# Convolution in-projections of a hybrid decoder trunk by Strassen's algorithm, with mixer outputs kept in DRAM

## Chip, cores and metric

The kernel runs on one core of a Trainium2 chip. The metric is the device time of one execution in microseconds. All inputs and outputs are float32 in DRAM.

## What is computed

A trunk of four layers is applied to one prompt of 1024 rows and to 8 decoding sequences of 4 rows each (model width 1024). Every layer modulates its input by vectors computed from a condition c (`adaln`), runs a mixer and closes with a gate, a residual and a layer norm. Layers 0 and 3 mix by a gated short convolution, layer 1 by an RG-LRU block, layer 2 by differential attention. What the change touches is the first product of the convolution layers, `u @ w_in`.

```python
def adaln(c, w, b):
    m = (jax.nn.silu(c) @ w + b)[:, None, :]
    shift, scale, gate = jnp.split(m, 3, axis=-1)
    return shift, scale, gate

def short_conv_mixer(u, buf, w_in, conv_w, w_out):
    h, bg, cg, z = jnp.split(u @ w_in, 4, axis=-1)
    y, new_buf = causal_dwconv(cg * h, buf, conv_w)
    return (jax.nn.silu(z) * bg * y) @ w_out, new_buf
...
    up = xp * (1.0 + scp) + shp
    us = xs * (1.0 + scs) + shs
...
    xp = layer_norm(DEEPNORM_ALPHA * xp + gtp * op, ln_g[i], ln_b[i])
```

## The kernel before

Activations lie transposed: 8 units (`u[k]`) of 128 features by NT = 1056 columns, 1024 of the prompt and 32 of the sample rows. Each number is held as two float32r parts, hi and lo, side by side in one unit, and every weight likewise. A product of two such numbers is three matmuls (hi·hi, w hi·u lo, w lo·u hi), so one output tile over 8 feature blocks is 24 matmuls (`gemm_chunk`, L123). The columns go in three chunks, `CH` = 384, 384 and 288.

`conv_layer` loops over 8 output blocks i. Each block takes four slices of 128 columns of `w_in`, in the order q = 2, 0, 3, 1 (cg, h, z, bg). `part` runs one chunk of one slice and finishes it: ScalarE copies cg out of PSUM (L397), VectorE multiplies (p, L405), ScalarE and VectorE do the convolution with width 3 (L413, L415), ScalarE applies silu (L429), VectorE forms the two last products (L431, L432), and `split` writes the result as hi and lo into `y[i]` (L92, L93), which the out-projection reads. In layer 0, block 0 goes chunk by chunk over all four slices, because its input columns come chunk by chunk.

Weights come by `load_w` (through `conv_weights`): a DMA of 512 KB on SP's queue into a raw buffer (L106, ring of two), a cast by ScalarE (hi, L107) and a subtraction by VectorE (lo, L108) into a ring of two weight tiles. All DMAs shown here go through SP's queue, in order. After each slice `filler` may put out one `ada_piece`: four DMAs of 512 KB from `w_ada` (L185, in the same raw ring) with 16 matmuls (L191), a copy and four transposes, for the gates of this and the next layer. In layer 0 there are 8 such pieces, in layer 3 none. After the layer, `boundary` runs the out-projection (tile `op`), the residual and the norm.

PSUM has 8 banks in four groups (P 3, Q 1, R 3, U 1), handed out in turn by `deal`. A scheduler sets the order of instructions per engine at build time from the order in the code, the buffers and its own costs; each engine then works its queue in order.

Of the kernel before, what the change touches and what calls it, by code (L numbers as in the profile page):

```python
# [21 lines left out]
T = 1024  # L22
NB = 8
# [9 lines left out]
CH = [(0, 384), (384, 384), (768, 288)]  # L33
TILES = [[(0, 128), (128, 128), (256, 128)], [(0, 128), (128, 128), (256, 128)], [(0, 128), (128, 128), (256, 32)]]
NPG = 16
SAMPLE_COST = NB * (32 * 430 + 8 * 890 + 620 + 4 * 430 + 16 * 400 + 300 + 300.0)
LAM_INIT = 0.8 - 0.6 * math.exp(-0.3 * 2)

# [6 lines left out]
class Trunk:  # L45
# [324 lines left out]
    def conv_weights(self, l, y, s):  # L370
        wv = self.a["a_w_in"][l // 3].rearrange("(k p) f -> p k f", p=128)
        i, q = s // 4, (2, 0, 3, 1)[s % 4]
        dst = None
        if l == 0 and s in (2, 3):
            dst = y[KB - 4 + s]
# [4 lines left out]
    def conv_layer(self, l, u, y, filler, wts=()):  # L380
# [4 lines left out]
        first = len(wts) > 0  # L385

        def ld(s):
            if s < 4 * KB and s not in wts:
                wts[s] = self.conv_weights(l, y, s)

        def part(i, q, c, wt, cg, yc, sz, p, psv):
            c0, n = CH[c]
            npr = min(n, T - c0)
            ps = self.gemm_chunk(wt, u, c, f"in{l}_{i}_{q}_{c}")
            if q == 2:
                cg[c] = cg.get(c) or self.sm(f"cg{l}_{i}_{c}")
                nc.scalar.copy(cg[c][:, :n], ps[:, :n])  # L397
            elif q == 0:
                yc[c] = yc.get(c) or self.sm(f"yc{l}_{i}_{c}")
                t = p[c] = self.sm(f"p{l}_{i}_{c}")  # L400
# [10 lines left out]
                w = [self.pv[:, i, R_CW + 3 * j + k : R_CW + 3 * j + k + 1] for k in range(3)]  # L411
                o = yc[c]
                nc.scalar.mul(o[:, :npr], t[:, 0:npr], w[0])  # L413
                for k in (1, 2):
                    nc.vector.scalar_tensor_tensor(  # L415
                        o[:, :npr], t[:, k : k + npr], w[k], o[:, :npr], ALU.mult, ALU.add
                    )
                if npr < n:
                    ov = o[:, npr:n].rearrange("p (b t) -> p b t", b=NB)
                    nc.vector.tensor_scalar(ov, psv[:, :, 0:4], w[0], None, ALU.mult)  # L420
                    for k in (1, 2):
                        nc.vector.scalar_tensor_tensor(ov, psv[:, :, k : k + 4], w[k], ov, ALU.mult, ALU.add)
                    nc.gpsimd.tensor_copy(stage[:, i, 0:2], t[:, npr : npr + 2])
                    nc.gpsimd.tensor_copy(
                        stage[:, i, 2:18].rearrange("p (b t) -> p b t", b=NB), psv[:, :, 4:6]
                    )
# [8 lines left out]
        ld(0)  # L435
        for i in range(KB):
            cg, yc, sz, p = {}, {}, {}, {}
# [3 lines left out]
            if first and i == 0:  # L441
                for s in range(4):
                    ld(s)
                for c in range(3):
                    for s, q in enumerate((2, 0, 3, 1)):
                        part(i, q, c, wts[s], cg, yc, sz, p, psv)
                ld(4)
                for s in range(4):
                    wts.pop(s)
                    filler(s, 4 * KB)  # L450
                continue
            pair = l == 3 and i == 0
            if pair:
                for s in range(3):
                    ld(s)
                for c in range(3):
                    for s, q in enumerate((2, 0)):
                        part(i, q, c, wts[s], cg, yc, sz, p, psv)
                for s in range(2):
                    wts.pop(s)  # L460
            for k, q in enumerate((2, 0, 3, 1)):
                if pair and k < 2:
                    continue
                s = 4 * i + k
                ld(s + 1)
                wt = wts.pop(s)
                if k < 3:
                    t, d = (("cg", cg), ("yc", yc), ("sz", sz))[k]
                    for c in range(3):
                        d[c] = self.sm(f"{t}{l}_{i}_{c}")  # L470
                for c in range(3):
                    part(i, q, c, wt, cg, yc, sz, p, psv)
                filler(s, 4 * KB)
# [849 lines left out]
    def run(self):  # L1323
# [65 lines left out]
        self.conv_layer(0, A, B, filler_for((0, 4), (0, 5), 1), wts)  # L1389
        boundary(0, a["a_w_out"][0], B, A)  # L1390
        if self.layers > 1:
            ct.__exit__(None, None, None)
# [33 lines left out]
            cms = [ct] + cms  # L1426
            boundary(2, a["d_w_out"][0], A, B)
        if self.layers > 3:
            self.conv_layer(3, A, B, filler_for())
# [84 lines left out]
```

## Time and profile before

| what | us |
|---|---|
| median of 3 runs (lowest to highest) | 2508.14 (2506.17 to 2513.81) |
| the profiled execution's own time | 2500.39 |
| span of its profile | 2498.6 |
| mean granted TensorE clock in it | 0.991 |
| layer 0, in-projections (tile in, first to last start) | 34 to 448, with ada pieces between |
| layer 3, in-projections | 2033 to 2384 |

One execution was profiled; its span runs from the first to the last instruction, and 1.8 us of its time lie outside. PE is TensorE's matmul side, PEld its weight loads, which overlap; DVE is VectorE, ACT ScalarE, POOL GpSimd, SP the engine whose queue issues DMAs. L123 is line 123 of the kernel before. A matmul's own duration overlaps with the next one's, so distances between starts tell what one costs. "Idle before" is the time an engine stood still ahead of an instruction, with what released it.

### The profile page before, as it was taken

What the parts mean: (1) busy time and instruction counts of PE and PEld (TensorE: products, weight loads), DVE (VectorE), ACT (ScalarE), POOL (GpSimd) and SP (SyncE); (2) the same over time, 40 slices, a digit from 0 to 9 for tenths busy, and PEclk for the clock granted to TensorE, in tenths of its full rate; (3) what the DMA queues carried; (4) which work ended last, traced back from release to release, by engine and by line L of the source; (5) the groups of instructions that cost most, each with busy time, mean ns of one, the idle gap of its engine ahead of it and who ended that gap; (6) DMA issues with size and microseconds to landing.
All of it is one profiled execution on the core that took longest, in us unless ns stands there. A gap on an engine that the chain in (4) does not pass through costs nothing.

```text
span 2498.6 us, 41729 instructions
## 1 busy us (share of the span) xinstructions
PE 2419.9 (97%) x16142; PEld 2102.1 (84%) x16142; DVE 1210.6 (48%) x2702; ACT 894.3 (36%) x1837; POOL 195.4 (8%) x330
## 2 busy tenths in 40 slices
PE   8999999999999999999999989988998999999997
PEld 5999999998888897777778966666776999999997
DVE  5323232466466546333333257777874552332355
ACT  4212221246455424112222257677762342222210
POOL 0000000001001000000000023232200000000000
PEclk9999999999999999999999999999999999999999
DMA  9223222433444524344588478899877321111132
GB/s 328 78 85 93 77 78 86 132 100 105 143 133 128 154 70 150 95 153 153 176 276 275 149 216 257 262 267 251 273 253 233 99 68 51 43 44 51 43 118 84
DMA packets 276715, 364.13 MB, mean 146 GB/s; under 512 B 15085, under 2 KB 192622, under 8 KB 276518
## 3 DMA queue, kind: packets, MB, share of 16 engines
q1 hardware_dynamic: 276518, 361.48, 46.3%
q8 instruction: 127, 2.08, 0.4%
q14 instruction: 70, 0.57, 0.1%
HBM read 313.94 MB, written 47.48 MB: 145 GB/s over the span
## 4 chain that ended last, share of the span: by engine, by line
PE 86%; DMA 9%; DVE 2%; ACT 2%; issue 1%; SPq 1%; POOL 0%; DVEq 0%; ACTq 0%; POOLq 0%
PE in L123 30%; PE op L123 15%; PE qk L796 10%; PE xb L123 4%; PE z L123 4%; PE skt L1131 4%; DMA kp<-cache_k 3%; PE ada L191 2%; PE zz L123 2%; PE S L912 2%; PE sps L1112 2%; PE g L628 2%; PE sacc L1171 2%; PE pv L1005 2%; DMA vp<-cache_v 1%; DMA tok<-kd 1%
## 5 line engine op out<-in xcount | busy, mean ns | idle before, releaser
L123 PEld LDWEIGHTS in<-ua,wi 128*128 128x128 f32 x4392 | 707.7, 188 | 22.5 <-issue 14.3
L123 PE MATMUL in<-ua,wi 128*128 128x384 f32 (+1 forms) x4392 | 722.4, 324 | 1.3 <-ACT wi L107 0.7
L796 PE MATMUL qk<-wq,ua 128*128 128x512 f32 x1152 | 289.6, 402 | 0.5 <-ACT qkr L800 0.5
L796 PEld LDWEIGHTS qk<-wq,ua 128*128 128x128 f32 x1152 | 211.4, 189 | 61.4 <-issue 11.4
L1131 PE MATMUL skt<-ident,kp 128*128 128x128 f32 x1024 | 143.8, 276 | 15.3 <-DMA kp<-cache_k 13.9
L1131 PEld LDWEIGHTS skt<-ident,kp 128*128 128x128 f32 x1024 | 116.1, 141 | 41.8 <-issue 11.6
L964 ACT ACTIVATE P<-S,rr 128x512 f32<-128x512 f32 (+2 forms) x192 | 111.1, 586 | 32.7 <-DVE rr L952 22.6
L912 PE MATMUL S<-ks,qhl 128*128 128x512 f32 (+2 forms) x384 | 109.3, 388 | 9.1 <-ACT P L964 8.8
L1135 DVE COPY sk<-skt 128x512 f32<-128x512 f32 x128 | 86.8, 686 | 58.5 <-PE skt L1131 38.0
L283 DVE SCALAR_TENSOR_TENSOR r<-op,gate,xr 128x384 f32<-128x384 f32 (+1 forms) x96 | 54.2, 569 | 121.5 <-PE op L123 85.4
L431 DVE TENSOR_TENSOR sz<-in,sz 128x384 f32<-128x384 f32 (+1 forms) x48 | 25.1, 524 | 176.9 <-PE in L123 176.5
L1135 ACT COPY sk<-skt 128x512 f32<-128x512 f32 x128 | 75.1, 590 | 78.7 <-PE skt L1131 51.9
L123 PEld LDWEIGHTS z<-ub,wrz 128*128 128x128 f32 x576 | 92.5, 188 | 11.7 <-issue 10.1
L123 PE MATMUL zz<-ua,wz 128*128 128x384 f32 (+1 forms) x576 | 102.0, 329 | 0.0
L123 PEld LDWEIGHTS zz<-ua,wz 128*128 128x128 f32 x576 | 92.2, 188 | 7.1 <-issue 7.0
L123 PE MATMUL z<-ub,wrz 128*128 128x384 f32 (+1 forms) x576 | 98.2, 326 | 0.0
L123 PEld LDWEIGHTS xb<-ub,wrx 128*128 128x128 f32 x504 | 81.0, 188 | 12.7 <-issue 9.2
L123 PE MATMUL xb<-ub,wrx 128*128 128x384 f32 (+1 forms) x504 | 87.9, 328 | 0.0
L191 PE MATMUL ada<-wada,ct 128*32 128x512 f32 x384 | 83.0, 624 | 3.6 <-DMA wada<-w_ada 2.4
L1171 PE MATMUL sacc<-vp,pt 128*32 128x256 f32 x1024 | 73.9, 395 | 12.6 <-DMA vp<-cache_v 10.8
L123 PE MATMUL op<-ub,ua 128*128 128x384 f32 (+1 forms) x504 | 85.5, 326 | 0.0
L123 PE MATMUL op<-ua,ub 128*128 128x384 f32 (+1 forms) x504 | 85.3, 325 | 0.0
(415 smaller groups left out, 3733.3 us busy)
## 6 DMA issues: line engine op xcount, KB each, us to landing
kp<-cache_k SPq DMA_DIRECT2D x128, 512.0 KB, 4.7
vp<-cache_v SPq DMA_DIRECT2D x128, 512.0 KB, 4.9
wada<-w_ada SPq DMA_DIRECT2D x96, 512.0 KB, 4.7
xa<-xat SPq DMA_DIRECT2D x64, 192.0 KB, 2.2
xr<-xa SPq DMA_DIRECT2D x64, 192.0 KB, 3.6
wi_2r<-a_w_in SPq DMA_DIRECT2D x16, 512.0 KB, 4.1
wi_0r<-a_w_in SPq DMA_DIRECT2D x16, 512.0 KB, 4.2
wi_3r<-a_w_in SPq DMA_DIRECT2D x16, 512.0 KB, 4.1
```

The lines of the kernel that those rows point to most:

```text
L123: nc.tensor.matmul(ps[:, :n], wt[:, wp, k], self.ucols(units[k], up, c), start=i == 0, stop=i == 3 * KB - 1)
L191: nc.tensor.matmul(ps[c : c + 32, :], self.ct[:, k], wts[k // 2][:, k % 2], start=k < 4, stop=k >= 4, tile_position=(0, c),)
L283: nc.vector.scalar_tensor_tensor(r[:, :npr], ps[:, :npr], gate[:, d, 0:1], xt[:, :npr], ALU.mult, ALU.add)
L628: nc.tensor.matmul(ps[:, :n], wt[:, wp, q, k, m * 128 : (m + 1) * 128], self.ucols(y[2 * i + k], up, c), start=j == 0, stop=j == 5,)
L796: nc.tensor.matmul(ps, u[k][:, c0 : c0 + 128], wq[n, k // 2][:, wp, k % 2], start=i == 0, stop=i == 3 * KB - 1)
L912: nc.tensor.matmul(st[:, o : o + w], qs[h, g][:, part, s, 128 * qj : 128 * qj + 128], ks[h][:, s, l0 : l0 + w], start=part == 0, stop=part ...
L964: nc.scalar.activation(p[:, o : o + w], x["S"][s][i][:, :w], AF.Exp, scale=-1.0, bias=rr[:, 6 + s : 7 + s], accum_out=rr[:, c : c + 1])
L1005: nc.tensor.matmul(x["pv"], x["w"][kb // 4][:, j : j + 128], V[h][:, kb], start=kb == 0, stop=kb == qb)
L1112: nc.tensor.matmul(ps[32 * g : 32 * g + 32, :n], qbs[b % 2][:, 2 * g + hl], kt[hl][:, g], start=hl == 0, stop=hl == 1, tile_position=(0, 3 ...
L1131: nc.tensor.transpose(tp[:, 128 * g : 128 * g + 128], pg[j][:, 128 * h : 128 * h + 128], ident)
L1135: e(kt[:, :, 128 * j : 128 * j + 128], tp.rearrange("p (g t) -> p g t", g=4))
L1171: nc.tensor.matmul(acc[32 * g : 32 * g + 32, :], pts[0][:, 128 * (p % 4) + 32 * g : 128 * (p % 4) + 32 * g + 32], v[:, 256 * g : 256 * g + ...
```

## The change

The in-projections of blocks 1 to 7 are done by Strassen's algorithm (Winograd's form with 7 products). Two slices of one block make a pair: kind 0 is (cg, h), kind 1 is (z, bg). The 2x2 matrices are: the two slices by two halves of the input features (4 blocks each), and the two halves of the features by two halves of the columns (HB = 528). Seven steps take the place of eight; one step is two halves of 12 matmuls with 264 columns, accumulated into PSUM banks X (two), Y (two) and Z (two).

- Block 0 stays direct. It stores its result to DRAM (`yd[0]`, L496). While it runs, `conv_sums` forms the column-side sums of the units (GpSimd adds hi and lo back together, L393; VectorE subtracts, L397 to L400) and splits them into `y`, which is free until the end.
- `conv_pair_weights` loads the two raw slices (L425), casts the first one whole (`direct`, wa), forms four sums on VectorE (L435 to L438) and splits them (`early`, `late`, `last`; casts L413, subtractions L414). These six stages of the next pair are put out after steps 0, 1, 2, 3, 5 and 6 of a pair.
- `pair` runs the seven steps (matmuls L603), copies banks out on ScalarE (p1, u2, p5, u3, L586) and adds on VectorE (L610, L622) and GpSimd (L619).
- There are 13 pairs per layer; (z, bg) of block 7 stays direct, in four chunks of 264. In that last half block `ret` reads the seven stored results back (L677) and splits them into `y`.
- `swap(True)` closes the pool of temporaries and opens one for the pairs; `swap(False)` reverses it.

Block 7's result goes straight into `y[7]`. Lines in the diff and the orders below are those of the changed kernel.

```diff
@@ -372,12 +373,89 @@
+    def conv_sums(self, l, u, e, d):
...
+        for x in (u[d], u[d + 4]):
+            t = self.xct(f"cs{l}_{d}_{len(b)}")
+            xf = x.bitcast(F32)
+            nc.gpsimd.tensor_tensor(t, xf[:, :NT], xf[:, NT:], ALU.add)
+            b.append(t)
+        (b11, b12), (b21, b22) = ((t[:, :HB], t[:, HB:]) for t in b)
+        tt = nc.vector.tensor_tensor
+        tt(b11, b12, b11, ALU.subtract)
+        tt(b12, b22, b12, ALU.subtract)
+        tt(b22, b22, b11, ALU.subtract)
+        tt(b21, b21, b22, ALU.subtract)
+        for t, o in zip(b, (e[d], e[d + 4])):
+            self.split((o[:, :NT], o[:, NT:]), t, NT)
...
+    def conv_pair_weights(self, l, i, kind, raw):
...
+        def split(dst, src):
+            nc.scalar.copy(dst[:, 0], src)
+            nc.vector.tensor_tensor(dst[:, 1], src, dst.bitcast(F32)[:, 0], ALU.subtract)
...
+        def sums():
...
+            tt(a[:, :4], a[:, :4], b[:, :4], ALU.subtract)
+            tt(s2, b[:, 4:], a[:, :4], ALU.subtract)
+            tt(b[:, :4], b[:, :4], b[:, 4:], ALU.add)
+            tt(a[:, 4:], a[:, 4:], s2, ALU.subtract)
+        def early():
+            split(ring("S2"), st["s2"])
+            split(ring("S1"), st["b"][:, :4])
+        def late():
+            split(ring("S3"), st["a"][:, :4])
+            split(ring("S4"), st["a"][:, 4:])
+        def last():
...
+            split(w[:, :, :4], st["b"][:, 4:])
...
+        return [load, direct, sums, early, late, last], get
...
@@ -408,69 +486,223 @@
-                self.split((self.ucols(y[i], 0, c), self.ucols(y[i], 1, c)), yc[c][:, :n], n)
+                nc.sync.dma_start(yd[i][:, c0 : c0 + n], yc[c][:, :n])
...
+        swap(True)
...
+        steps = (
+            ("Y", col(u, 4, 0)), ("X", col(u, 0, 0)), ("X", col(y, 4, 1)), ("Z", col(y, 0, 0)),
+            ("X", col(y, 0, 1)), ("Z", col(u, 4, 1)), ("X", col(y, 4, 0)))
+        QH = HB // 2
...
+        def pair(i, kind, get, o, stages, fills):
...
+            for n, (tgt, mov) in enumerate(steps):
...
+                for jj in range(2):
+                    m = 0
+                    for k in range(4):
+                        for wp, up in ((0, 0), (0, 1), (1, 0)):
+                            nc.tensor.matmul(
+                                B[tgt][jj][:, :QH], w[n][:, wp, k], mov[k](jj, up), start=new and m == 0, stop=m == 11,
+                                skip_group_check=not new)
...
+                if n == 1:
+                    p1 = copies(f"p1{nm}", B["X"])
...
+                elif n == 2:
+                    u2 = copies(f"u2{nm}", B["X"])
...
+                if n in (0, 1, 2, 3, 5, 6) and stages:
+                    stages.pop(0)()
+                if n in (2, 5) and fills:
+                    filler(fills.pop(0), 4 * KB)
...
+        todo = [(i, k) for i in range(1, KB) for k in range(2)][:-1]
...
+                nc.vector.tensor_tensor(yc[:, :NT], yc[:, :NT], o, ALU.mult)
+                nc.sync.dma_start(yd[i], yc[:, :NT])
...
+        def ret():
+            if back:
+                k = back.pop(0)
+                t = wide(f"yb{l}_{k}")[:, :NT]
+                nc.sync.dma_start(t, yd[k])
+                self.split((y[k][:, :NT], y[k][:, NT:]), t, NT)
...
+        for s, q in ((2, 3), (3, 1)):
+            wt = w2[4 * i + s]
+            for c in range(4):
...
+        swap(False)
```

The order of instructions, at three places. First SP's queue (DMA issues in their order) at the end of block 0 in layer 0, before and after; `wada_4_n` and `wada_5_n` are weights of ada pieces 4 and 5, `wi_i_q` a slice of block i, `wra` and `wrb` the two slices of a pair, `yd` the stored result.

```order
L185 DMA wada_4_2_952<-w_ada 128x2x512
L185 DMA wada_4_4_956<-w_ada 128x2x512
L185 DMA wada_4_6_960<-w_ada 128x2x512
L106 DMA wi_1_0r<-a_w_in 128x8x128
L106 DMA wi_1_3r<-a_w_in 128x8x128
L106 DMA wi_1_1r<-a_w_in 128x8x128
L185 DMA wada_5_0_1255<-w_ada 128x2x512
L185 DMA wada_5_2_1259<-w_ada 128x2x512
```

```order
L496 DMA yd_588<-yc_0_1_765 128x384
L186 DMA wada_4_4_1004<-w_ada 128x2x512
L496 DMA yd_588<-yc_0_2_891 128x288
L186 DMA wada_4_6_1008<-w_ada 128x2x512
L186 DMA wada_5_0_1393<-w_ada 128x2x512
L186 DMA wada_5_2_1397<-w_ada 128x2x512
L425 DMA wra_1_0_1025<-a_w_in 128x8x128
L425 DMA wrb_1_0_1027<-a_w_in 128x8x128
```

Before, the last three loads of ada piece 4 are followed by three slices of block 1, whose first slice was loaded ahead. Now the stores of block 0 stand among the ada loads, and the first pair's two slices come after the first two loads of piece 5.

Second, ScalarE in a running pair, here the second pair of block 2 with the next pair's weights; `p_` and `u_` are copies of banks, `wa`, `wsS` and `wd` casts of weights.

```order
L586 COPY p_2_00_1611<-inX_2_0_1585 128x264
L586 COPY p_2_01_1613<-inX_2_0_1586 128x264
L413 CAST wa_2_1_1617<-wra_2_1_1581 128x1024
L586 COPY u_2_00_1644<-inX_2_0_1585 128x264
L586 COPY u_2_01_1646<-inX_2_0_1586 128x264
L586 COPY p_2_00_1679<-inZ_2_0_1653 128x264
L413 CAST wsS_2_1_1683<-wst_2_1_1648 128x512
L586 COPY p_2_01_1681<-inZ_2_0_1654 128x264
L413 CAST wsS_2_1_1686<-wrb_2_1_1583 128x512
L586 COPY u_2_00_1713<-inX_2_0_1585 128x264
```

The cast of the next pair's first weights (`wa_2_1`) stands between the copies after step 2 (p) and those after step 3 (u); none of it was there before.

Third, ScalarE at the start of the pairs in layer 3; `cs_` are the column-side sums, `wst` the sum S2 of the first pair's weights.

```order
L413 CAST wd_1_0_23882<-wrb_1_0_23860 128x512
L93 CAST ub1b_22208<-cs_1_0_23758 128x1056
L586 COPY p_1_00_23945<-inX_1_0_23919 128x264
L93 CAST ub1a_22201<-cs_1_1_23760 128x1056
L586 COPY p_1_01_23947<-inX_1_0_23920 128x264
L413 CAST wsS_1_0_23870<-wst_1_0_23865 128x512
L413 CAST wsS_1_0_23873<-wrb_1_0_23860 128x512
```

The casts of the last sums (`cs_1_0`, `cs_1_1`) and one bank copy (`p_1_00`) now stand ahead of the cast of S2.

## Rows read from the trace of the kernel before

**Rows 1.** Page, parts 1 and 4: engines' busy time, and the chain that ended last.

```profile
PE 2419.9 (97%) x16142; PEld 2102.1 (84%) x16142; DVE 1210.6 (48%) x2702; ACT 894.3 (36%) x1837; POOL 195.4 (8%) x330
...
PE 86%; DMA 9%; DVE 2%; ACT 2%; issue 1%; SPq 1%; POOL 0%; DVEq 0%; ACTq 0%; POOLq 0%
PE in L123 30%; PE op L123 15%; PE qk L796 10%; PE xb L123 4%; PE z L123 4%; PE skt L1131 4%; DMA kp<-cache_k 3%; PE ada L191 2%; PE zz L123 2%; PE S L912 2%; PE sps L1112 2%; PE g L628 2%; PE sacc L1171 2%; PE pv L1005 2%; DMA vp<-cache_v
```

**Rows 2.** Busy time by window, one of layer 3, one of layer 0.

```profile
core 0: us, PE busy (x) PEld busy (x) DVE busy (x) ACT busy (x) POOL busy (x), PEclk, DMA share, GB/s
2110.00:2160.00 50.00, 50.00 (x311) 50.00 (x310) 15.22 (x26) 10.13 (x17) 1.12 (x6) 1.00 0.18 51
100.00:200.00 100.00, 100.00 (x611) 92.55 (x611) 32.75 (x59) 21.75 (x35) 2.24 (x12) 1.00 0.32 96
```

**Rows 3.** Timeline of TensorE: end of block 0 in layer 0, and layer 3.

```profile
start us, us, engine line op out<-in xcount [idle before <-releaser]
69.74 8.53 PE L123 MATMUL in<-ua,ub 128*128 128x384 f32 x48
78.11 6.51 PE L123 MATMUL in<-ua,wi 128*128 128x288 f32 x48
84.46 6.51 PE L123 MATMUL in<-ua,ub 128*128 128x288 f32 x48
90.89 1.07 PE L191 MATMUL ada<-wada,ct 128*32 128x512 f32 x8
91.89 6.24 PE L123 MATMUL in<-ua,wi 128*128 128x384 f32 x34
...
2099.68 284.37 PE L123 MATMUL in<-ua,wi 128*128 128x384 f32 x1767
2383.89 1.03 PE L364 MATMUL cs3ps<-ident,cstage 128*18 128x128 f32 x8
```

**Rows 4.** Timeline of TensorE in layer 2, transposes of 128 columns.

```profile
1352.31 1.47 PE L1131 MATMUL skt<-ident,kp 128*128 128x128 f32 x12
1353.53 0.99 PE L123 MATMUL zz<-ua,wz 128*128 128x288 f32 x5
```

**Rows 5.** Timeline of VectorE, last products of block 0, layer 0.

```profile
91.07 0.46 DVE L431 TENSOR_TENSOR sz<-in,sz 128x288 f32<-128x288 f32 x1 [4.31 <-PE in L123]
91.56 0.46 DVE L432 TENSOR_TENSOR yc<-yc,sz 128x288 f32<-128x288 f32 x1
```

**Rows 6.** DMA issues: count, KB each, median us from issue to landing.

```profile
wada<-w_ada SPq DMA_DIRECT2D x96, 512.0 KB, 4.7
wi_2r<-a_w_in SPq DMA_DIRECT2D x16, 512.0 KB, 4.1
...
V<-vd SPq DMA_DIRECT2D x8, 512.0 KB, 8.4
wq_3r<-d_w_in SPq DMA_DIRECT2D x6, 512.0 KB, 7.1
```

**Rows 7.** Windows (columns as in rows 2) and TensorE's timeline after an idle stretch.

```profile
10.00:20.00 10.00, 8.64 (x44) 2.92 (x40) 4.95 (x32) 1.46 (x3) 0.00 (x0) 1.00 1.04 395
579.00:583.00 4.00, 4.00 (x21) 4.00 (x22) 1.49 (x5) 3.97 (x8) 0.76 (x4) 0.65 0.69 230
...
578.92 4.73 PE L123 MATMUL xb<-ub,wrxx 128*128 128x288 f32 x24 [3.11 <-ACT xb_0s L586]
583.49 3.36 PE L123 MATMUL xb<-ub,wrx 128*128 128x288 f32 x24
```

**Rows 8.** ScalarE's groups: busy us, mean ns of one, idle before.

```profile
L107 ACT CAST wi<-wi_0r 128x1024 fp32r<-128x1024 f32 x16 | 16.9, 1053 | 22.2 <-PE in L123 22.2
L933 ACT CAST ua<-yt 128x512 fp32r<-128x512 f32 x16 | 9.9, 622 | 1.4 <-DVE yt L931 1.4
L397 ACT COPY cg<-in 128x288 f32<-128x288 f32 x16 | 6.4, 400 | 40.7 <-PE in L123 40.7
L413 ACT ACTIVATE yc<-p,pv 128x384 f32<-128x384 f32 x32 | 19.7, 616 | 101.8 <-DVE p L405 100.6 <-DVE u L252 1.3
```

**Rows 9.** VectorE's groups.

```profile
L108 DVE TENSOR_TENSOR wi<-wi_2r,wi 128x1024 fp32r<-128x1024 f32 x16 | 19.6, 1225 | 61.9 <-ACT wi L107 61.8
L934 DVE TENSOR_TENSOR ua<-yt,ua 128x512 fp32r<-128x512 f32 x16 | 14.0, 878 | 1.3 <-ACT ua L933 1.3
```

**Rows 10.** GpSimd's largest addition.

```profile
L906 POOL TENSOR_TENSOR qhl<-tok,qhl 128x1024 fp32r<-128x1024 f32 x16 | 39.2, 2452 | 100.9 <-ACT qhl L905 100.7
```

**Rows 11.** Waits of TensorE: us in total, times, longest us.

```profile
PE ada L191 <- DMA wada<-w_ada: 2.4, 7, 0.7
```

**Rows 12.** Groups of the weight loads (PEld), 100 to 500 us.

```profile
L123 PEld LDWEIGHTS in<-ua,wi 128*128 128x128 f32 x1977 | 318.3, 188 | 18.5 <-issue 12.6 <-ACT sz L429 5.9
```

More of the change, by code (lines that the diff above doesn't have):

```diff
@@ L35 @@
 NPG = 16
+HB = NT // 2
 SAMPLE_COST = NB * (32 * 430 + 8 * 890 + 620 + 4 * 430 + 16 * 400 + 300 + 300.0)
@@ L387, in ld @@
         def ld(s):
-            if s < 4 * KB and s not in wts:
+            if s not in wts:
                 wts[s] = self.conv_weights(l, y, s)
@@ L410, in part @@
                     )
[L411 to L426, printed above, removed]
+                conv(i, t, yc[c], psv, npr, n)
             elif q == 3:
@@ L440, in conv_layer @@
             nc.gpsimd.tensor_copy(psv[:, :, 0:2], sc)
-            if first and i == 0:
-                for s in range(4):
-                    ld(s)
-                for c in range(3):
[L445 to L473, printed above, removed]
+            return psv
@@ new lines, in conv_layer, with more @@
+        sums = [0, 1, 2, 3] if first else [0, 2, 3, 1]
+        def more():
+            if sums:
+                self.conv_sums(l, u, y, sums.pop(0))
+        cg, yc, sz, p = {}, {}, {}, {}
+        psv = past(0)
+        if first:
+            for s in range(4):
+                ld(s)
+            for c in range(3):
+                for s, q in enumerate((2, 0, 3, 1)):
+                    part(0, q, c, wts[s], cg, yc, sz, p, psv)
+                    if c == 2:
+                        more()
+            for s in range(4):
+                filler(s, 4 * KB)
+        else:
+            for s in range(3):
+                ld(s)
+            for c in range(3):
+                for s, q in enumerate((2, 0)):
+                    part(0, q, c, wts[s], cg, yc, sz, p, psv)
+            for s in range(2):
+                wts.pop(s)
+            ld(3)
+            for s, q in ((2, 3), (3, 1)):
+                if s == 2:
+                    for c in range(3):
+                        sz[c] = self.sm(f"sz{l}_0_{c}")
+                for c in range(3):
+                    more()
+                    part(0, q, c, wts[s], cg, yc, sz, p, psv)
@@ new lines, in conv_layer, with raw, wide, narrow @@
+        wts.clear()
+        swap(True)
+        def raw(shape, name):
+            return self.fp.tile(shape, F32, tag="wr", bufs=2, name=name) if l == 0 else self.raw(shape, name)
+        def wide(name):
+            return self.fp.tile([128, NT + 2], F32, tag="cx", bufs=4, name=name)
+        def narrow(name):
+            if l == 0:
+                return self.fp.tile([128, HB // 2], F32, tag="cpy", bufs=8, name=name)
+            return self.sm(name)[:, : HB // 2]
+        def col(units, d0, half):
+            return [
+                lambda jj, up, k=k: units[d0 + k][:, up * NT + HB * half + jj * (HB // 2) :][:, : HB // 2]
+                for k in range(4)]
@@ new lines, in conv_layer @@
+        self.deal(tp="QU", mm="PR")
+        back = list(range(KB - 1))
+        def ret():
[4 more added lines that the diff above has]
+                self.split((y[k][:, :NT], y[k][:, NT:]), t, NT)
+        i = KB - 1
+        gate = [narrow(f"szl{l}_{c}") for c in range(4)]
+        for s, q in ((2, 3), (3, 1)):
+            wt = w2[4 * i + s]
+            for c in range(4):
+                cs = slice(QH * c, QH * c + QH)
+                ps = self.mm(f"in{l}_{i}_{q}_{c}")
+                m = 0
+                for k in range(KB):
+                    for wp, up in ((0, 0), (0, 1), (1, 0)):
+                        nc.tensor.matmul(
+                            ps[:, :QH], wt[:, wp, k], u[k][:, up * NT + QH * c : up * NT + QH * c + QH],
+                            start=m == 0, stop=m == 3 * KB - 1)
+                        m += 1
+                if s == 2:
+                    nc.scalar.activation(gate[c], ps[:, :QH], AF.Silu)
+                    ret()
+                else:
+                    oc = yc[:, cs]
+                    nc.vector.tensor_tensor(gate[c], ps[:, :QH], gate[c], ALU.mult)
+                    nc.vector.tensor_tensor(oc, oc, gate[c], ALU.mult)
+                    self.split((y[i][:, cs], y[i][:, NT + QH * c : NT + QH * c + QH]), oc, QH)
+                ret()
+            filler(4 * i + s, 4 * KB)
@@ L1388, in run, with swapper, swap @@
             self.modulate(0, c, [self.load_x(3 * c + i) for i in range(3)], A)
-        self.conv_layer(0, A, B, filler_for((0, 4), (0, 5), 1), wts)
+        def swapper(l, old, **kw):
+            cur = [old]
+            def swap(fast):
+                cur[0].__exit__(None, None, None)
+                cm, p = self.pool(f"{'fast' if fast else 'tmpb'}{l}", reuse_waits="tile", **kw)
+                cur[0] = cm
+                if fast:
+                    self.fp = p
+                else:
+                    self.tmp = p
+            return cur, swap
+        yd = [dpool.tile([128, NT], F32, name=f"yd{k}") for k in range(KB)]
+        cur, swap = swapper(0, ct, side="right")
+        self.conv_layer(0, A, B, filler_for((0, 4), (0, 5), 1), wts, swap, yd)
+        ct = cur[0]
         boundary(0, a["a_w_out"][0], B, A)
@@ L1428, in run @@
         if self.layers > 3:
-            self.conv_layer(3, A, B, filler_for())
+            cur, swap = swapper(3, cms[0])
+            self.conv_layer(3, A, B, filler_for(), (), swap, yd)
+            cms[0] = cur[0]
             boundary(3, a["a_w_out"][1], B, A)
```

115 lines of the change are left out of this document (110 added, 5 removed).

## The prediction

> **What bounds the kernel now.** I read the page's first part and its chain of waits first [rows 1]. TensorE has matmuls under way in 97% of the span, and the chain that ended last lies on it for 86%. The other engines are busy for 8 to 48%. The input projections of the two convolution layers (line 123, tile "in") are 30% of that chain by themselves. Then I read the two stages that are changed, as windows [rows 2]: in both of them TensorE is busy without a gap at full clock while VectorE, ScalarE, GpSimd and the DMA engines have two thirds of their time free. So here a matmul less is time saved, if three things hold: a smaller matmul is proportionally shorter, everything added fits beside TensorE, and the first pair of each layer has its data in time. Those are the three parts of the sum.
>
> **Price of a matmul.** Busy time of one matmul (335 to 446 ns) says nothing, as they overlap. I take the distance of starts in the timeline [rows 3]. From 69.74 to 78.11 us there are 48 matmuls of 384 columns: 8.37/48 = 174.4 ns. From 78.11 to 84.46 us there are 48 of 288: 132.3 ns. The long row of layer 3 checks it: 284.21/1767 = 160.8 ns, and two chunks of 384 with one of 288 make 160.4. No row has 264 columns. Below lies the transpose of 128 columns, (1353.53 − 1352.31)/12 = 102 ns each [rows 4], above lie 132.3 ns. So the price is between 102 and 132.3. The nearest row is 288; the line through 288 and 384 (0.4385 ns a column, 6.0 ns fixed) gives 121.8 ns, which I take. I let it move by 2 ns either way for the range, since 24 columns is a quarter of the distance that the line spans.
>
> **The pairs.** One pair is two feature slices. Before: 2 × 3 × 24 = 144 matmuls, 48 × (174.4 + 174.4 + 132.3) = 23.09 us. After: 7 steps × 2 halves × 12 = 168 matmuls of 264, 168 × 121.8 = 20.46 us. That is 2.63 us less, and with 13 pairs in each of 2 layers **−68.4 us**. The half block that stays direct now goes in four chunks of 264: 192 × 121.8 = 23.39 instead of 23.09, twice: **+0.6**. That the change does not do this is excluded: the order shows the 14 groups of 12.
>
> **Start of layer 0.** Before, TensorE goes straight from block 0 (ends 90.89) through one piece of the gate (ada) into block 1 [rows 3]. After, SP's queue has the stores of block 0's result, then three loads of ada weights, and only then the two loads for the first pair. The second store waits for VectorE's last product, which ends at 92.0 [rows 5]. Two buffers hold the ada weights, so two of the loads wait for a landing (4.7 us [rows 6]) and a use. My estimate from these: the pair's first load is issued at about 97.8; with 2 MB under way at some 395 GB/s (that is what the stretch at 10 us moved [rows 7]) it lands at about 103; ScalarE's cast 1.05 [rows 8] and VectorE's remainder 1.23 [rows 9] end at 105.2. In these 14.3 us TensorE has about 5 us of work: ada pieces, and the 8 products of each first group that need the high part alone. So 9 us are lost. After an idle stretch of 3.11 us the trace shows TensorE at a lower granted clock: 0.65 from 579 to 583, 24 matmuls of 288 in 4.57 us instead of 3.17 [rows 7]; I add 1.4. Together **+10** (6 if the ada loads are handed out at once, 16 if also the sums of the activations are late). Those sums are next in line: 8 additions of 1056 columns on GpSimd, 8 × 2.5 = 20 us by its 1024-column row [rows 10], begin near 78 and with their splits end about 103; the third step needs them, at 105.2 + 5.8. They cost nothing only because the weights are later still.
>
> **Start of layer 3.** There block 0 runs slice by slice, the first pair's weights come in good time, and the sums are spread over it. But in ScalarE's order the cast for step 3 (S2) stands behind a copy of step 2's bank and behind a cast of 1056 columns. From the end of step 2: copy 0.4, cast 1.1, cast of 512 0.62, VectorE's remainder 0.88 [rows 8, 9] = 3.0, and VectorE has its own queue there: **+3.5** (0 to 8).
>
> **Smaller terms.** In layer 0 the second half of an ada piece follows 42 matmuls after the first, 5.1 us; before it was 34, 6.2 us. The load lands after 4.7 [rows 6], and in all TensorE waited 2.4 us for these loads before, at 7 places [rows 11]: **+1** (0 to 3). The out-projections begin after results were read back from DRAM; SP's queue puts 7 × 0.54 MB ahead of their first weights: **+1** (0 to 3) for both layers.
>
> **What I cost at nothing**, and its cover. A pair adds on ScalarE 8 copies (0.40 by the 288 row), five casts of 512 and one of 1024, one pass over the block: 8 × 0.40 + 5 × 0.62 + 1.05 + 1.2 = 8.6 us. VectorE: 9 operations of 512, 8 of 264, three of 1024: at most 9 × 0.88 + 8 × 0.46 + 3 × 1.23 = 15.3 us [rows 8, 9]. Both are under the 20.5 us of TensorE's pair, which hides them; without that cover VectorE would be the next bound, at 15.3. DMA adds 4.3 MB stored and 3.8 read per layer, while in the stage the DMA engines are busy for a third at most [rows 2]. The weights are the same bytes. A pair's first weights are issued about 19 us into the pair before it and land about 3.4 us into their own pair; the cast's place in ScalarE's queue is behind step 2, at 5.9, a slack of 2.5.
>
> **The sum.** −68.4 + 0.6 + 10 + 3.5 + 1 + 1 = −52.3. The profiled execution took 2500.4 (span 2498.6 and 1.8 around it), so it would become 2448; it lies 7.7 under the median of the runs, 2508.1. Against the median: **2456 us**.
>
> **The rivals.**
> *The weight load sets the pace.* Each matmul brings a load of 128 columns, and the load unit shows 188 ns apiece [rows 12], busy for all 50 us of a window in layer 3 [rows 2]. The change makes more loads (168 for 144). (a) If every load cost the mean spacing of 160.8 ns, a pair would take 27.0 us, the half blocks 30.9: 26 × 3.9 + 2 × 7.8 + 15.5 = +133, 2641 us. The Trainium skill, page "Perfetto Trace Analysis", section "Identifying the Most-Contended Engine", says to judge TensorE by the busy share of weight loads and not of matmuls; by that page the unit is full already, and adding loads can only cost. The rows speak against it: 48 loads followed each other at 132.3 ns between 78.11 and 84.46 [rows 3], so 160.8 is no floor. Chance 0.02. (b) A floor just at 132.3 is not refuted by any row of the same shape: then a pair takes 22.23, the gain is 26 × 0.86 − 2 × 2.3 − 15.5 = 2, **2506 us**. Against it: 128-column matmuls come 102 ns apart [rows 4]. Chance 0.06.
> *Each pair stalls a little.* A bank's copy or a late remainder costs 1 us a pair: +26, **2482 us**. Between two uses of the X banks lies a step of 24 matmuls, 2.9 us, for copies of 0.4, so I give it 0.09.
> *Slower: ScalarE's queue held by a weight load.* It works in order. The cast of the next pair's weights stands ahead of the copies that free the X banks for step 5. Should the load land late, cast, copies and TensorE stand still together. Price: 1 us a pair for every us over the slack of 2.5 + 2.9. Break-even is 2.0 us a pair, measurably slower from 2.3, so the load must take about 11.8 us; at 3 us a pair the time is +26, **2534 us**. For it: loads of 512 KB that took 7.1 and 8.4 us where much was under way [rows 6]. Against it: in these stages they take 4.1. Chance 0.07.
>
> **How the numbers follow.** My case 0.76, stalls 0.09, floor at 132.3 0.06, held queue 0.07, pace of loads 0.02. Its own range: 120 ns and the low bounds of the starts give 2456 − 8 − 9, 124 ns and the high bounds +10 and +14: 2439 to 2480. The range of 2438 to 2484 takes in the stalls and leaves out the last three, 0.15. A measurement can tell 0.3%, 7.5 us, from no change: faster 0.85, same 0.07 (the floor, and a queue held by about 2 us), slower 0.08.
>
> **What would show it.** Starts of 264-column matmuls 121.8 ns apart and a pair in 20.5 us would show the first term right; 132 would show rival (b). A gap on TensorE near 95 to 105 us, ended by the weights of the first pair, shows the start of layer 0. A gap of 3 to 4 us near 2065 ended by the cast of S2 shows the start of layer 3. A gap that returns in each pair would make the forecast wrong, and its releaser tells which rival it is: a copy of X alone (stalls), a load through a cast (slower).

## The result and the profile after

The changed kernel takes 2477.88 us (median of 4 runs, 2473.66 to 2479.05), before 2508.26 (2506.17 to 2513.81); the ratio is 0.9872 with an interval of 0.9852 to 0.9892. It is faster, by 30.4 us where 52 were forecast, and inside the range of 2438 to 2484. The profiled execution took 2479.05 us.

The page of the changed kernel, parts 1 and 4, answers to [rows 1]:

```profile
PE 2364.2 (95%) x16862; PEld 2041.9 (82%) x16862; DVE 1429.6 (58%) x2972; ACT 998.7 (40%) x2059; POOL 284.0 (11%) x384
...
PE 82%; DMA 9%; DVE 5%; ACT 2%; issue 1%; SPq 1%; POOL 0%; DVEq 0%; ACTq 0%; POOLq 0%
```

TensorE is busy 56 us less, but its share of the chain fell and VectorE's rose from 2 to 5%: some of the gain went to a new wait. I cut both traces at marks that all kernels here share: the last transpose of a convolution layer's input (xt) and the first matmul of its out-projection (op).

| stretch, us | before | changed | difference |
|---|---|---|---|
| layer 0, last xt to first op | 382.97 | 366.92 | −16.05 |
| layers 1 and 2, from there to the last xt of layer 3 | 1580.46 | 1594.15 | +13.69 |
| layer 3, last xt to first op | 355.47 | 335.90 | −19.57 |

The two changed stages gained 35.6 us. The middle, which the change leaves alone, is another matter and comes at the end of the experiments.

TensorE's timeline of the changed kernel, answering to [rows 3]; first a running pair of layer 0, then one of layer 3 from its first step to the next pair's:

```profile
177.56 3.09 PE L603 MATMUL inX<-ub,wd 128*128 128x264 f32 x24
180.49 3.08 PE L603 MATMUL inY<-ua,wa 128*128 128x264 f32 x24
...
2093.87 3.09 PE L603 MATMUL inY<-ua,wa 128*128 128x264 f32 x24
...
2114.32 3.09 PE L603 MATMUL inY<-ua,wa 128*128 128x264 f32 x24
```

24 matmuls of 264 columns take 2.93 us, 122 ns each, and a pair 20.45 us. The forecast had 121.8 and 20.46. So the pairs gave their whole 13 × 2 × 2.64 = 68.6 us, the two half blocks cost 0.6, and 68.6 − 0.6 − 35.6 = **32.4 us went elsewhere**, not 15.5. The waits of TensorE in the changed kernel (us in total, times, longest) tell where; [rows 11] had 2.4 us in the first of them:

```profile
PE ada L192 <- DMA wada<-w_ada: 18.2, 12, 10.3
...
PE inX L603 <- ACT wsS L413: 6.7, 1, 6.7
...
PE in L124 <- DVE wi L109: 3.1, 2, 2.0
PE in L124 <- ACT cg L475: 2.4, 1, 2.4
```

Of the 18.2 us in the first line 14.4 lie at the start of the pairs in layer 0, and of the 3.1 in the third 2.0 at their start in layer 3; the other two lie there whole. The start in layer 0, TensorE's timeline:

```profile
84.90 6.51 PE L124 MATMUL in<-ua,ub 128*128 128x288 f32 x48
91.34 1.07 PE L192 MATMUL ada<-wada,ct 128*32 128x512 f32 x8
96.10 1.92 PE L192 MATMUL ada<-wada,ct 128*32 128x512 f32 x4 [3.70 <-DMA wada<-w_ada]
108.35 1.92 PE L192 MATMUL ada<-wada,ct 128*32 128x512 f32 x4 [10.32 <-DMA wada<-w_ada]
...
117.22 0.75 PE L603 MATMUL inY<-ua,wa 128*128 128x264 f32 x4 [0.95 <-ACT wa L413]
```

Block 0 ends at 91.3, near the 90.9 of before, and the first pair starts at 117.2 instead of the 105.2 forecast. SP's queue shows the loads behind one store:

```profile
103.91 0.32 SPq L496 DMA_DIRECT2D yd<-yc  x1
104.32 6.36 SPq L186 DMA_DIRECT2D wada<-w_ada  x3
110.77 0.42 SPq L425 DMA_DIRECT2D wra<-a_w_in  x1
```

The store waits for block 0's last product, at 103.88 and not at 92.0 as in [rows 5]. Why is seen in the timelines of GpSimd and VectorE laid side by side:

```profile
88.47 2.66 POOL L393 TENSOR_TENSOR cs<-ua 128x1056 f32<-128x1056 f32 x1 [2.96 <-DVE ub L94]
...
92.94 2.80 POOL L393 TENSOR_TENSOR cs<-ua 128x1056 f32<-128x1056 f32 x1 [1.21 <-DVE ub L94]
...
101.16 2.40 POOL L393 TENSOR_TENSOR cs<-ua 128x1056 f32<-128x1056 f32 x1
```

```profile
88.72 2.97 DVE L397 TENSOR_TENSOR cs<-cs 128x528 f32<-128x528 f32 x1
91.61 1.25 DVE L94 TENSOR_TENSOR ub<-cs,ub 128x1056 fp32r<-128x1056 f32 x1
92.78 0.69 DVE L398 TENSOR_TENSOR cs<-cs,cs 128x528 f32<-128x528 f32 x1
93.40 0.41 DVE L483 TENSOR_TENSOR p<-in,cg 128x256 f32<-128x256 f32 x1
...
93.83 2.48 DVE L399 TENSOR_TENSOR cs<-cs,cs 128x528 f32<-128x528 f32 x1
...
96.78 0.69 DVE L400 TENSOR_TENSOR cs<-cs 128x528 f32<-128x528 f32 x1
...
101.55 2.33 DVE L495 TENSOR_TENSOR yc<-yc,sz 128x288 f32<-128x288 f32 x1
```

A subtraction of 528 columns takes 0.69 us alone and 2.5 to 3.0 beside an addition on GpSimd: it ends some 0.6 us after that does. The last product itself, 0.46 us before [rows 5], took 2.33 in this way. The product p at 93.40, which has one operand in PSUM, took 0.41 beside such an addition. And GpSimd waits in turn for VectorE (ub, L94), for a buffer. The two take turns, and block 0's products stand in VectorE's queue among them.

Layer 3 shows the same: TensorE finishes the first two steps, then stands 6.66 us for the cast of S2, whose sum VectorE forms at 2075.11, behind the last column sums (VectorE's timeline follows TensorE's).

```profile
2045.36 4.74 PE L124 MATMUL in<-ua,ub1b 128*128 128x288 f32 x24 [2.40 <-ACT cg L475]
2049.94 0.51 PE L124 MATMUL in<-ua,wi 128*128 128x384 f32 x2
...
2067.00 2.85 PE L603 MATMUL inX<-ua,wa 128*128 128x264 f32 x22
2076.50 1.25 PE L603 MATMUL inX<-ub1a,wsS 128*128 128x264 f32 x4 [6.66 <-ACT wsS L413]
```

```profile
2073.94 1.26 DVE L94 TENSOR_TENSOR ub1a<-cs,ub1a 128x1056 fp32r<-128x1056 f32 x1 [1.19 <-ACT ub1a L93]
2075.11 0.68 DVE L436 TENSOR_TENSOR wst<-wrb,wra 128x512 f32<-128x512 f32 x1
```

### The profile page after: what moved, and what is told of

The parts are those of the page before. It is cut to its first block, busy times and chain, and to the rows that moved or that the text cites. A ratio compares the mean times of both kernels' runs of the same rounds, so it can differ in the third digit from the quotient of the medians.

```text
span 2477.3 us, 44030 instructions
## 1 busy us (share of the span) xinstructions
PE 2364.2 (95%) x16862; PEld 2041.9 (82%) x16862; DVE 1429.6 (58%) x2972; ACT 998.7 (40%) x2059; POOL 284.0 (11%) x384
## 4 chain that ended last, share of the span: by engine, by line
PE 82%; DMA 9%; DVE 5%; ACT 2%; issue 1%; SPq 1%; POOL 0%; DVEq 0%; ACTq 0%; POOLq 0%
PE op L124 15%; PE inX L603 12%; PE qk L1028 10%; PE inZ L603 6%; DMA kp<-cache_k 4%; PE xb L124 4%; PE zz L124 4%; PE z L124 4%; PE skt L1363 4%; PE inY L603 3%; PE ada L192 2%; PE S L1144 2%; PE sps L1344 2%; PE g L860 2%; PE pv L1237 2%; PE sacc L1403 2%
## 5 line engine op out<-in xcount | busy, mean ns | idle before, releaser
L1028 PEld LDWEIGHTS qk<-wq,ua 128*128 128x128 f32 x1152 | 210.7, 188 | 60.0 <-issue 12.5
L192 PE MATMUL ada<-wada,ct 128*32 128x512 f32 x384 | 87.8, 640 | 19.4 <-DMA wada<-w_ada 18.2
L619 POOL TENSOR_TENSOR u<-u,p 128x264 f32<-128x264 f32 x52 | 40.4, 779 | 469.3 <-ACT u L586 440.0
L1032 ACT ACTIVATE qkr<-qk 128x512 f32<-128x512 f32 x48 | 28.4, 597 | 157.0 <-PE qk L1028 93.7
L1237 PEld LDWEIGHTS pv<-V,wt 128*128 128x128 f32 x576 | 75.6, 198 | 10.9 <-issue 2.5
```

Source lines behind the costliest of these rows:

```text
L192: nc.tensor.matmul(ps[c : c + 32, :], self.ct[:, k], wts[k // 2][:, k % 2], start=k < 4, stop=k >= 4, tile_position=(0, c),)
L1028: nc.tensor.matmul(ps, u[k][:, c0 : c0 + 128], wq[n, k // 2][:, wp, k % 2], start=i == 0, stop=i == 3 * KB - 1)
L1237: nc.tensor.matmul(x["pv"], x["w"][kb // 4][:, j : j + 128], V[h][:, kb], start=kb == 0, stop=kb == qb)
```

## The experiments

Theory A: the column sums (GpSimd and VectorE) hold VectorE's queue, and through it stores, loads and the units of step 3. Theory B, the forecast's: the order of SP's and ScalarE's queues delays the first pair's weights. The stages of the table above, for all runs, in us:

| kernel | layer 0 | layer 3 | layers 1, 2 | time, us |
|---|---|---|---|---|
| before, three traces | 382.97 | 355.46 to 355.47 | 1580.5, 1583.0, 1589.4 | 2508.26 |
| changed, two traces | 366.92, 368.54 | 335.90, 335.65 | 1594.2, 1591.6 | 2477.88 |
| sums all on VectorE | 364.09 | 331.56 | 1599.6 | 2476.45 |
| pair's weights first | 371.30 | 334.66 | 1584.2 | 2473.10 |
| no sums | 356.29 | 319.99 | 1594.0 | 2452.58 |
| GpSimd's additions alone | 356.19 | 322.43 | 1597.4 | 2458.14 |
| VectorE's sums alone | 357.24 | 320.19 | 1602.6 | 2462.41 |
| one more direct half block | 360.89 | 329.59 | 1590.5 | 2470.13 |
| the same, sums all on VectorE | 350.48 | 323.52 | 1600.4 | 2452.81 |

The times are medians, except those of the two partial sums (additions alone, VectorE's sums alone), which are one execution each. Where one number stands for a stage, it is from one trace; layer 0 differs by 1.6 us between the two traces of the changed kernel, so stage differences of that size say little.

**No sums.** `conv_sums` is not called, and the steps read `u`:

```diff
-        sums = [0, 1, 2, 3] if first else [0, 2, 3, 1]
+        sums = []
...
-            ("Y", col(u, 4, 0)), ("X", col(u, 0, 0)), ("X", col(y, 4, 1)), ("Z", col(y, 0, 0)),
-            ("X", col(y, 0, 1)), ("Z", col(u, 4, 1)), ("X", col(y, 4, 0)))
+            ("Y", col(u, 4, 0)), ("X", col(u, 0, 0)), ("X", col(u, 4, 1)), ("Z", col(u, 0, 0)),
+            ("X", col(u, 0, 1)), ("Z", col(u, 4, 1)), ("X", col(u, 4, 0)))
```

> The column sums are left out in both layers; steps 3, 4, 5 and 7 of a pair read the units themselves in their place, so the layers' values are not the reference's. Everything else stays. Theory A: block 0's last product in layer 0 ends at about 92 and the first pair starts at 103 to 106, as the prediction's 10 us had it (10 to 13 us less than the changed kernel); in layer 3 the wait of 6.7 us for S2 and the small ones near 2045 to 2053 go (9 to 14 us less); 19 to 27 us faster in all. Rival B (queues and weights alone): layer 0 within 3 us of the changed kernel, layer 3 within 4; under 7 us faster in all.

Layer 0 is 10.6 us shorter than in the changed kernel, layer 3 15.9, the time 25.3 us (2452.58; ratio to before 0.9771, 0.9752 to 0.9791). The first pair started at 101.43, a little earlier than expected. Layer 3 gave more than the 9 to 14 us expected. Theory A holds; of the 32.4 us lost, 26.5 belong to the sums. What is left, 5.9 us (7.3 lost in layer 0, 1.5 gained in layer 3), is the most that can be B's share, where the forecast had put all 15.5.

**Which part of the sums?** Two runs part them. In one only the additions stay (subtractions and splits removed, steps read `u`); in the other the additions go and VectorE subtracts the high parts of the units:

```diff
-            nc.gpsimd.tensor_tensor(t, xf[:, :NT], xf[:, NT:], ALU.add)
...
-        tt(b11, b12, b11, ALU.subtract)
-        tt(b12, b22, b12, ALU.subtract)
-        tt(b22, b22, b11, ALU.subtract)
-        tt(b21, b21, b22, ALU.subtract)
+        tt(b11, x12, x11, ALU.subtract)
+        tt(b12, x22, x12, ALU.subtract)
+        tt(b22, x22, b11, ALU.subtract)
+        tt(b21, x21, b22, ALU.subtract)
```

> Of the column sums only GpSimd's eight additions per layer stay; the subtractions and splits are left out, and steps 3, 4, 5 and 7 read the units themselves, so the layers' values are not the reference's. It parts the loss into what GpSimd's additions do to VectorE and what VectorE's own sums do. If the additions alone hold VectorE (an instruction with two operands in SBUF waits beside them): block 0's last product in layer 0 ends after 97 and the stage of layer 0 is 5 us or more longer than without sums. If VectorE's own work is the load: the product ends by 94, layer 0 and layer 3 are each within 3 us of the run without sums; 2450 to 2458 us.

> The converse: GpSimd's additions are left out, VectorE's subtractions read the high parts of the units alone, and all subtractions and splits stay (so the sums lack the low parts, and the values are not the reference's to full precision). If GpSimd's additions and the waits beside them are the loss: layer 0 is 9 us or more shorter than in the changed kernel and the wait for S2 in layer 3 falls under 2 us. If VectorE's 21 us of own sums and casts per layer are: layer 0 is 3 to 6 us shorter and S2 still waits 3 us or more.

Each run met the condition by which its expectation blames the other part, so neither is the loss alone. With the additions alone the stages are −0.1 and +2.4 us from the run without sums, with VectorE's part alone +1.0 and +0.2. Together they cost 10.6 and 15.9. The run with the additions alone has a limit: nothing reads their results, so they run back to back and the last ends at 85 us, before block 0's last products, where in the changed kernel the last ends at 103.6. It tells what they cost by themselves, not what they cost among VectorE's sums. Busy time in the two starts (75 to 108 and 2034 to 2076 us; columns as in [rows 2]), first the changed kernel, then without sums, additions alone, VectorE's part alone:

```profile
75.00:108.00 33.00, 19.33 (x130) 16.52 (x128) 32.80 (x35) 9.64 (x13) 17.83 (x10) 0.82 0.16 48
2034.00:2076.00 42.00, 31.43 (x198) 30.46 (x196) 40.67 (x51) 15.79 (x22) 18.04 (x10) 0.91 0.08 26
```

```profile
75.00:108.00 33.00, 28.25 (x179) 23.48 (x178) 10.36 (x22) 6.00 (x11) 0.74 (x4) 0.84 0.35 106
```

```profile
75.00:108.00 33.00, 27.54 (x178) 23.48 (x177) 18.79 (x27) 7.24 (x14) 10.94 (x9) 0.90 0.34 106
```

```profile
75.00:108.00 33.00, 24.14 (x149) 18.13 (x148) 19.56 (x34) 8.60 (x12) 2.35 (x4) 0.93 0.41 124
```

VectorE (third pair of numbers) is busy 10.4 us of 33 without sums, 18.8 and 19.6 with one part, and 32.8, all of it, with both. It counts as busy also while it stands beside an addition, as the subtractions of 2.5 to 3.0 us above; and with the additions alone five operations more fall into its window. The chain can be worked out: for one of the four groups of units two additions at 2.45 (the 1024-column row of [rows 10], about the 2.40 of the shortest here), four subtractions at 0.69 and two remainders at 1.25, one after the other, are 10.2 us; four groups 41 us. In layer 0 two additions and a subtraction were done by 69.7; what was left is 35 us by the same prices and took until 108.4, 39 us, with block 0's own operations between. In layer 3 three additions and a subtraction came earlier, as the units came; the rest, with block 0's own operations between, filled VectorE from 2035 to 2075.2 but for 1.2 us.

**Sums all on VectorE.**

```diff
-            nc.gpsimd.tensor_tensor(t, xf[:, :NT], xf[:, NT:], ALU.add)
+            nc.vector.tensor_tensor(t, xf[:, :NT], xf[:, NT:], ALU.add)
```

> Only the eight additions hi + lo per layer go from GpSimd to VectorE. Theory A (the column sums hold VectorE's queue ahead of block 0's last products, because each GpSimd addition takes 2.4 to 2.8 us and VectorE's subtractions beside one take 2.3 to 3.0 us instead of 0.7): the subtractions of 528 columns all take about 0.7 us, the additions about 1.25 us, block 0's last product in layer 0 ends by 98 instead of 103.9, the wait of 6.7 us for S2 in layer 3 shrinks by 4 us or more; 5 to 12 us faster than the changed kernel in all. Rival B (the order of the queues of SP and ScalarE is what delays the first pair's weights, as the prediction had it): within 3 us of the changed kernel, or slower as VectorE has 10 us more work per layer.

Subtractions took 0.70 us throughout, additions 1.25, and block 0's last product ended at 96.9. The stages are 2.8 and 4.3 us shorter, but the marks at which they begin come 1.2 us later in their layers. In the time it does not show (2476.45, ratio 0.9861, 0.9839 to 0.9883): there it came out as rival B had it, within 3 us of the changed kernel, and not 5 to 12 us faster. And the wait for S2 grew to 8.6 us, against A's number:

```profile
2075.92 1.25 PE L603 MATMUL inX<-ub1a,wsS 128*128 128x264 f32 x4 [8.56 <-ACT wsS L413]
```

By the same working the chain is still 4 × 7.8 = 31 us, and all of it is now VectorE's. Taking GpSimd out is no cure as long as TensorE has nothing else to do.

**The pair's weights first.** In layer 0 the calls of `filler` for block 0 are moved behind the first pair's weight stages.

```diff
-            for s in range(4):
-                filler(s, 4 * KB)
...
         for f in stages:
             f()
+        if first:
+            for s in range(4):
+                filler(s, 4 * KB)
```

> In layer 0 the ada pieces that follow block 0 are put out after the first pair's weight stages, so SP's queue issues the first pair's two loads ahead of the ada loads. Theory A: the loads still stand behind the last store of block 0, which waits for VectorE until about 104; the first 264-column matmul comes at about 110 instead of 117, so 4 to 7 us faster, and layer 3 is as it was. Rival B (SP's order alone): the loads go at about 92.5, the first pair starts at 98 to 101, and layer 0 is 13 to 17 us shorter.

Both theories missed. The scheduler left the ada loads ahead all the same, as SP's timeline shows, and TensorE waited 10.15 us for VectorE (sz) instead of for a load; layer 0 was 4.4 us longer than in the first trace of the changed kernel. The run says nothing on the order it was to test; what it shows is that moving the calls did not move the loads.

```profile
104.41 7.57 SPq L186 DMA_DIRECT2D wada<-w_ada  x4
112.07 0.42 SPq L425 DMA_DIRECT2D wra<-a_w_in  x1
```

**Cover instead of less work.** Direct work needs no sums. One more half block, (z, bg) of block 1, goes direct between block 0 and the pairs; its gate waits in `yd[1]`, is read back and multiplied after the pair (1, 0). Its weights and the first pair's two slices are loaded ahead of the second ada piece, the latter into the raw ring:

```diff
+                        if q in (2, 0):
+                            ld(6 + s)
...
+        stages, get = self.conv_pair_weights(l, 1, 0, self.raw)
+        stages.pop(0)()
+        for s, q in ((6, 3), (7, 1)):
...
+            for c, (c0, n) in enumerate(CH):
+                ps = self.gemm_chunk(wt, u, c, f"in{l}_1_{q}_{c}")
...
+                    nc.sync.dma_start(yd[1][:, c0 : c0 + n], sz[c][:, :n])
...
-        todo = [(i, k) for i in range(1, KB) for k in range(2)][:-1]
+        todo = [(1, 0)] + [(i, k) for i in range(2, KB) for k in range(2)][:-1]
```

> One more half block (z, bg of block 1) is done direct between block 0 and the pairs, its weights and the first pair's two slices being loaded ahead of the ada loads of piece 5; 12 pairs per layer instead of 13, the rest as in the changed kernel. Theory A (the starts are lost to the column sums on VectorE, 16 us in each layer by the run without them, and TensorE only lacks other work meanwhile): 23 us of direct work cover them; two pairs less give back 5.3 us, the starts return some 26 to 32; the two layers come to 55 to 62 us less than before, 20 to 28 us faster than the changed kernel, 2450 to 2458 us. Rival B (the sums, the stores and the loads only move behind the half block, as they wait for its buffers): the starts still cost 10 us or more in each layer, within 8 us of the changed kernel or slower.

> As the run with one more direct half block, and the additions hi + lo on VectorE instead of GpSimd. Theory A: with the sums covered it matters little where they are added; within 4 us of that run. Rival B (VectorE's queue still sets when the direct weights and the products come): VectorE gets 20 us more work in the two starts but no instruction beside a GpSimd addition; 5 us or more to either side.

With the additions left on GpSimd it took 2470.13 us (ratio 0.9838, 0.9811 to 0.9866), 8 us less than the changed kernel and 12 above what was expected at most; by the time that is what rival B had. The intervals of the two ratios overlap, but both stages are 6 us shorter. By the reckoning used above, with 12 pairs, the starts still cost 9.3 and 5.5 us. TensorE stood 6.45 us again right after block 0, now behind an operation of the convolution:

```profile
97.86 1.92 PE L192 MATMUL ada<-wada,ct 128*32 128x512 f32 x4 [6.45 <-ACT yc L501]
```

With the sums on VectorE as well it took **2452.81 us** (ratio 0.9765, 0.9739 to 0.9791), faster than both kernels and by 25 us than the changed one. My expectation that the place of the additions would not matter under cover was wrong, the two are 17 us apart: cover helps little as long as the covering work's own operations go through the VectorE queue that is full. From 75 to 108 us VectorE was busy 32.9 of 33 us with the additions on GpSimd, 28.7 without. TensorE's timeline of this last kernel at the start of layer 0, and its busy time there, have no gap left:

```profile
84.56 6.50 PE L124 MATMUL in<-ua,ub 128*128 128x288 f32 x48
90.99 1.05 PE L192 MATMUL ada<-wada,ct 128*32 128x512 f32 x4
91.97 5.52 PE L124 MATMUL in<-ua,wi 128*128 128x384 f32 x30
...
109.54 9.91 PE L124 MATMUL in<-ua,wi 128*128 128x384 f32 x61
119.29 3.09 PE L626 MATMUL inY<-ua,wa 128*128 128x264 f32 x24
```

```profile
75.00:108.00 33.00, 33.00 (x209) 28.82 (x208) 28.73 (x41) 12.56 (x18) 9.48 (x4) 1.00 0.35 100
```

Its two stages gained 64.4 us over before; 24 pairs at 2.64 less 0.6 make 62.8. The first marks come 0.9 and 1.2 us later in their layers than in before, which leaves 62.3: the starts cost next to nothing there (TensorE stood 1.3 us in that of layer 3).

**The middle.** Layers 1 and 2 were 13.7 us longer in the first pair of traces, nearly all of it in the attention over the caches. Both kernels were profiled again.

> The kernel before, profiled once more, unchanged. In the changed kernel's trace the layers 1 and 2, which the change leaves alone, took 13.8 us longer than in the first trace of before (from the end of layer 0 to the start of layer 3: 12 us of it in the attention over the caches). Theory N (executions differ there, whatever the kernel): this trace shows that stretch at least 5 us longer than the first trace of before did, and its span is 2503 to 2512. Rival C (the change causes it, through its DRAM tensors or later transfers): the stretch comes out within 2 us of the first trace, span 2498 to 2501.

> The changed kernel, profiled once more, unchanged, for the stretch from the last matmul of tile zz to the start of layer 3 (attention over the caches), which was 12.5 us longer in its first trace than in the first trace of before; over the other changed kernels it was 3 to 21 us longer, and 3 us longer in the second trace of before. Theory N (executions differ there): this trace differs from the first trace of the changed kernel by 4 us or more in that stretch while the two convolution layers agree within 1 us. Rival C (the change lengthens it by a fixed amount): within 3 us of 12.5 again.

> The kernel before, profiled a third time. Theory N: its stretch of attention over the caches lies anywhere between 0 and 15 us over its first trace. Rival C: within 4 us of its first two traces, so that all three stand below all but one of the changed kernels.

Before came to 1580.5, 1583.0 and 1589.4 us, the changed kernel to 1594.2 and 1591.6, seven variants of it to 1584.2 to 1602.6, while the stages that nothing disturbs repeat to 0.01 us in before (382.97 three times). So executions of one kernel differ there by 9 us, as theory N had it for before. The changed kernel's second trace did not bear N out: its attention differed by 3.0 us and not by 4 or more from the first, and its layer 0 by 1.6. And the nine traces with pairs lie 10 us above the three of before on average (1594.9 against 1584.3), which N does not explain. The waits show where most of it lies: TensorE waited 20, 25 and 29 us for the loads of the two caches in before, and 28 to 37 us in the nine others (24.7 and 32.5 on average). Why the loads come later, and whether the change causes it, is open. It is where 35.6 us gained in the stages became 30.4 between the medians, or 21.3 between the two first traces.

## Why the prediction was right or wrong

- **Price of a matmul and the pairs: right.** 122 ns and 20.45 us, as the line through the two shapes gave. Both floors of that rival are out. In layer 3 the load unit shows 220 of 220 us busy as it showed 50 of 50 before [rows 2], yet it now passes 1809 loads in 220 us, 8.2 a microsecond, where it passed 6.2.

```profile
2110.00:2330.00 220.00, 220.00 (x1810) 220.00 (x1809) 134.97 (x223) 81.95 (x164) 20.35 (x44) 1.00 0.24 70
```

  The rival whose rule came from the Trainium skill, page "Perfetto Trace Analysis", section "Identifying the Most-Contended Engine", is thereby out for this kernel: the busy share of the loads was full before and after and told nothing of what was left.
- **Steady pairs: right.** No gap returns in them. From that row a pair has 134.97 × 20.45/220 = 12.5 us of VectorE and 7.6 of ScalarE, under the 15.3 and 8.6 bounded. Neither the pair that stalls nor the held queue of ScalarE came.
- **Start of layer 0: right in kind, too small.** 68.6/2 − 0.3 − 16.05 = 18.0 us instead of 10 and 1 for the ada waits. The step that failed is the one that costed the sums at nothing: "8 × 2.5 = 20 us by its 1024-column row [rows 10], begin near 78 and with their splits end about 103 … They cost nothing only because the weights are later still." GpSimd's 20 us and VectorE's share were taken as lying beside each other; one after the other they are 41 by the working above, and in the trace they ended at 108.4. And the product at 92.0 was read from the trace of before as if the sums did not stand ahead of it in VectorE's queue. Without the sums the stage leaves 68.6/2 − 0.3 − 26.7 = 7.3 us for the loads, near the forecast's 10.
- **Start of layer 3: wrong by mechanism.** 14.4 us instead of 3.5. The sentence "the sums are spread over it" passed over that same chain, most of which fell together with block 0's own operations. The S2 cast does end the wait, as said, but it was late through VectorE's sum, not through ScalarE's copies. The three waits are 11.1 of the 14.4 us. The rest goes with a lower clock behind two of them, for which the forecast had no term here: from 2045.36 24 matmuls of 288 columns took 4.58 us instead of 3.17, at a granted clock of 0.68, and from 2076.50 28 of 264 took 6.16 instead of 3.42, at 0.52. Without sums the stage is 1.5 us better than the pairs alone explain, so the 3.5 was nothing.
- **Smaller terms:** the out-projections start on time in both layers (2339.23 to 2362.57 is the last half block without a gap, and op follows). The readback of results costs nothing. What a layer stores is 7 × 0.54 = 3.8 MB, as much as it reads, not 4.3.

That the range held is luck in part. Its centre missed by 22 us, of which the mis-sized starts are 17 and the rest lies in the middle. With a matmul at 122 ns as forecast, the high bounds of the starts reach to 2470 only; the room for a matmul of 124 ns, which was not needed, took in the other 8 us.

## What to carry to other kernels

When a change puts elementwise work on two engines that wait for each other, cost it as one chain, serially, and set that against the time TensorE has to spend meanwhile; then ask which products, stores and loads of the old work stand behind it in the same queue. A saving on the bound engine that needs a preparation is worth little until something else covers the preparation: here one half block kept direct, costing 2.6 us per layer, returned most of the loss once the additions were off GpSimd too, and 8 us with them there.

## What the runs showed of the hardware

I had not expected that VectorE's operations with two operands in SBUF and GpSimd's additions take turns. Beside an addition of 2.4 to 2.8 us a subtraction took 2.5 to 3.0 us; with no addition on GpSimd, in the run with the sums all on VectorE, each took 0.70. The Trainium skill says so, page "SBUF — State Buffer", section "SBUF: two separate sides": the two engines share a pair of ports as an exclusive lock, held for a whole instruction. The rows agree; by that page the forecast's 20 us of sums would have become the 41 worked out above, an estimate.

TensorE's granted clock was 0.82 on average in the start of layer 0 and 0.91 in that of layer 3. In layer 0 it was 1.00 (2.4 GHz) in block 0's last matmuls and 0.50 (1.2 GHz) from 96.1, after TensorE had stood 3.70 us: four ada matmuls of a group took 1.92 us there, where they took 1.05 at 1.00 in the kernel that does not stand there.
